# One value piece for two tiles, the scan's decays in two steps, and the last roots on ScalarE and VectorE, in a hybrid decoder trunk on one core

## The chip, the core and the metric

The kernel runs on one core of one Trainium2 chip. The core has five engines with their own instruction streams: TensorE (PE: matmuls, with weight loads shown apart as PEld), VectorE (DVE), ScalarE (ACT), GpSimd (POOL) and SyncE (SP, here only DMA issues). They meet through semaphores. The metric is the device time of one execution in microseconds (us); lower is better. Times shown are medians of several runs, and one further execution is recorded by the hardware profiler.

## What is computed

Two layers over 256 tokens of 1024 columns, then a final RMS norm. A layer normalises its input, multiplies it with one wide matrix `w_in`, runs three mixers on slices of the product (a Mamba-2 scan, attention in a sliding window with sinks, and forgetting attention), gates and projects each, adds the three, projects once more and adds the input. Cut to what the change touches:

```python
# per layer
h = rms_norm(x, norm_w[layer])
proj = jnp.einsum('bsd,de->bse', h, w_in[layer])
... c_q, c_k, c_v, c_f, c_z, gates = jnp.split(proj, split_at, axis=-1)

# the scan, in two chunks of 128 tokens, 16 heads in 4 groups
a_cum = jnp.cumsum(a_dt, axis=-1)
seg = a_cum[..., :, None] - a_cum[..., None, :]
decay = jnp.where(causal, jnp.exp(jnp.where(causal, seg, 0.0)), 0.0)
y_diag = jnp.einsum('bgrcls,bcsgrp->bclgrp', cb[:, :, None] * decay, x_dt)
y_off = jnp.einsum('bclgn,bcgrpn,bgrcl->bclgrp', cc, prev, jnp.exp(a_cum))

# the end
x = x + jnp.einsum('bsd,de->bse', merged, w_out[layer])
return rms_norm(x, final_norm_w)     # x * rsqrt(mean(x * x) + eps) * w
```

## The kernel before

**Precision and pieces.** Every float32 matrix of weights is cut in two: `hi`, rounded to the type fp32r, and `lo`, the rest. A product is the sum of three: activation-high by weight-high, activation-low by weight-high, activation-high by weight-low. Weights come in *pieces* of 256 or 512 columns (`class Piece`), each in *parts* of 512 KB: 4 blocks of 128 rows at 256 columns, or 2 blocks at 512. SyncE loads a part (L356), ScalarE makes its `hi` (L286, or L1389 in the opening stage), VectorE its `lo` (L287, or L1395). At most four parts (`AHEAD`) are split ahead; the next is fed when a matmul loop releases one (`release`, `feed`).

**The two ways through a piece.** The 256 tokens are two tiles of 128. `tok` takes one tile through all 8 row blocks into one bank of accumulators, and is called once for each tile; `tok2` (through `dense2`) takes both tiles by turns, four row blocks of one, four of the other, into two banks. There are three banks of the name mm. For activations that are wanted transposed, `both_sums` makes one *channel* of 128 columns: 8 matmuls of 512 moving columns and 8 of 256.

**Order.** In the opening stage the order on TensorE, VectorE, ScalarE and GpSimd is the program's own. From there on only TensorE's is; on the other engines a planner orders the instructions at compile time, by the order in which the program traces them among those that it takes to be ready. Small stages are generators: `launch` queues one, each `yield` names a delay in the kernel's own estimate of TensorE's time (`clock`, advanced by `mm`), and `pump`, called after each channel or half tile, enters those that are due. A call of `pin` keeps an instruction behind the one traced before it on its engine.

**The scan.** `ssd_group` runs four times in each layer. Its step behind the token "ssd" transposes the inputs on TensorE, scales them (L812), copies B (L817), makes the decays to the chunk's end (L819, L820, L822), then for both chunks four decay rows (L829) and one exponential (L831), and the scaled C (L835, L836). After `D_SSD` the second step multiplies the decays by the products of B and C (L848), and the third does the value products. The first group of a layer comes between channels of the convolution (`u_conv`: an eviction, an accumulating DMA, then `taps` with L773 on ScalarE and three L776 on VectorE, then a tanh L782 and L783) and the first projection.

**The value columns.** In layer one the forgetting attention's values are made by `u_cv`: the first 512 columns are two pieces of 256 (`cv0`, `cv1`), each with two calls of `tok` and an eviction (L956) that scales by the row's norm. They run right behind the opening stage.

**The last norm.** `out_end` adds the input (L1133), sums squares (L242, or on VectorE for the last piece, L1137) and scales by the final weights. For the third piece it makes the variance (L281) and calls `row_rsqrt2`: GpSimd raises it to the power -0.5 (L253), VectorE refines that by one step (L255, L257) and the row is scaled and stored (L1156, L1158).

Of the kernel before, what the change touches and what calls it, by code (L numbers as in the profile page):

```python
# [14 lines left out]
ALU = mybir.AluOpType  # L15
# [6 lines left out]
NEG = -1.0e30  # L22
EPS = 1e-6

D_SOFT, D_SOFT2, D_EVAC, D_SSD, D_SSD2 = 7.0, 3.0, 3.0, 8.0, 4.0
D_K, D_Q, D_QK, D_G0, D_FOX, D_BDMA, D_BIAS, D_BC, D_SSD3 = 6.0, 5.5, 2.0, 8.0, 0.0, 4.0, 2.6, 5.5, 1.0
D_GN1, D_GN2, D_CUM, D_H, D_M = 8.0, 13.5, 12.0, (4.8, 6.4), 5.0
BUDGET = 1.35
# [19 lines left out]
def hybrid_trunk(  # L48
# [198 lines left out]
        ts(v[:, 0:1], v[:, 0:1], 1.0 / D, EPS, op0=ALU.mult, op1=ALU.add)  # L247
        return v

    def row_rsqrt2(v):  # L250

        r0 = T("sm", [P, 8])
        nc.gpsimd.tensor_tensor(r0[:, 0:1], v, mhalf[:, 0:1], op=ALU.pow)  # L253
        a = T("sm", [P, 8])
        stt(a[:, 0:1], r0[:, 0:1], v, r0[:, 0:1], op0=ALU.mult, op1=ALU.mult)  # L255
        r = T("rs", [P, 8], bufs=4)
        stt(r[:, 0:1], a[:, 0:1], -3.0, r0[:, 0:1], op0=ALU.add, op1=ALU.mult)  # L257
        return r
# [540 lines left out]
    def ssd_group(y, g):  # L799
        yield lambda: not any(m[2] == 1 for m in waiting)  # L800
        yield "bcg"
        bcg = T("L4", [P, 4, S])
        nc.scalar.dma_start(bcg, y.cumd[4 * g:4 * g + 4, 0, :].partition_broadcast(P))
        yield D_BC
        yield "ssd"
        xdt = T("L2", [P, 2, 256])
        hs = slice(4 * g, 4 * g + 4)
        for t in range(2):
            p = pmx()
            for j in range(2):  # L810
                transpose(p[:, j * P:(j + 1) * P], y.xs[:, 2 * g + j, t * P:(t + 1) * P], ident)
            tt(xdt[:, t, :].rearrange("p (h d) -> p h d", h=4),  # L812
               p[:, 0:256].rearrange("p (h d) -> p h d", h=4), bc(y.dt[:, t, hs], 2, 64), op=ALU.mult)
        p = pmx()
        transpose(p[:, 0:P], y.bcT[:, g, 0:P], ident)
        bt = T("bt", [P, P])
        act(bt, p[:, 0:P], AF.Copy)  # L817
        ds = T("ds", [P, 4], bufs=2)
        tt(ds, bcg[:, :, P - 1], y.acum[:, 0, hs], op=ALU.subtract)  # L819
        act(ds, ds, AF.Exp)  # L820
        xds = T("L1", [P, 256])
        tt(xds.rearrange("p (h d) -> p h d", h=4), xdt[:, 0, :].rearrange("p (h d) -> p h d", h=4),  # L822
           bc(ds, 2, 64), op=ALU.mult)
        decs = []
        for c in range(2):
            tk = slice(c * P, (c + 1) * P)
            dec = T("L2", [P, 4, P])
            for h in range(4):
                stt(dec[:, h, :], bcg[:, h, tk], y.acum[:, c, 4 * g + h:4 * g + h + 1], negtri,  # L829
                    op0=ALU.subtract, op1=ALU.add)  # L830
            act(dec, dec, AF.Exp)  # L831
            decs.append(dec)

        cx = T("L2", [P, 4, P])
        act(cx, bcg[:, :, P:S], AF.Exp)  # L835
        tt(cx, cx, bc(y.bcT[:, 4 + g, P:S], 1, 4), op=ALU.mult)  # L836
        yield D_SSD
        tokens["bcg"] += 1

        p = pmx()  # L840
        mm(p[:, 0:256], bt, xds, start=True, stop=True)
        for c in range(2):
            tk = slice(c * P, (c + 1) * P)
            mm(p[:, 256 + c * P:384 + c * P], y.bcT[:, g, tk], y.bcT[:, 4 + g, tk], start=True, stop=True)
        st = T("st", [P, 256])
        act(st, p[:, 0:256], AF.Copy)
        for c in range(2):
            tt(decs[c], decs[c], bc(p[:, 256 + c * P:384 + c * P], 1, 4), op=ALU.mult)  # L848
        yield Half(D_SSD2)

        py = pmx()
        for c in range(2):
            for j in range(2):
                o = py[:, S * j + P * c:S * j + P * c + P]
                for s in range(c + 1):
                    for i in range(2):
                        h = 2 * j + i
                        hc = slice(64 * h, 64 * h + 64)
                        a, b = (xdt[:, c, hc], decs[c][:, h, :]) if s == 0 else (st[:, hc], cx[:, h, :])
                        mm(o[64 * i:64 * i + 64, :], a, b, start=(s == 0), stop=(s == c))  # L860
        for j in range(2):
            u = 2 * g + j
            stt(y.xs[:, u, :], y.xs[:, u, :], y.dsk[:, u:u + 1], py[:, S * j:S * j + S], op0=ALU.mult, op1=ALU.add)
        yield D_SSD3
        tokens["ssd"] += 1
# [81 lines left out]
    def u_cv(y, c, t, i=None):  # L947

        def f(w):
            p = tok(y.hTh, y.hTl, w, t)  # L950
            if y.cv is None:
                y.cv = T("L8", [P, 2, D])
            m = w.n if i is None else w.n - 16
            rn = 1.0 if y.rn is None else y.rn[:, t:t + 1]
            if i is None:
                finish(act(halves(y.cv[:, t, c:c + m]), p, AF.Copy, scale=rn))  # L956
            else:
                n = w.n // 2
                act(y.cv[:, t, c:c + n], p[:, 0, :], AF.Copy, scale=rn)
                finish(act(y.cv[:, t, c + n:c + m], p[:, 1, 0:m - n], AF.Copy, scale=rn))  # L960
                logits(y, t, i, p[:, 1, m - n:n])
            pump()
        return f

# [151 lines left out]
    def u_out2(y, c):  # L1116

        def f(w):
            def late():
                drain(8)  # L1120
                limit(None, True)
            drain(7)
            xo = [out_start(y, c, t, 0, w.n) for t in range(2)]
            none = lambda: None
            for t, p in enumerate(tok2(y.mh, y.ml, w, (none, late, none, none))):
                out_end(y, c, t, 0, w.n, xo[t], p)
            state["pin"] = False
        return f

    def out_end(y, c, t, i, n, xo, p):  # L1130
        sl = slice(c, c + n)
        with tc.high_priority():
            tt(halves(y.xn[:, t, sl]), p, halves(xo), op=ALU.add)  # L1133
            last = y.l + 1 == L
            if last and i == 2:
                junk = T("L2", [P, 512])
                nc.vector.tensor_tensor_reduce(out=junk[:, 0:n], in0=y.xn[:, t, sl], in1=y.xn[:, t, sl],  # L1137
                                               scale=1.0, scalar=0.0, op0=ALU.mult, op1=ALU.add,
                                               accum_out=y.ss[t][:, i:i + 1])
            else:  # L1140
                sum_sq(y.xn, t, c, y.ss[t][:, i:i + 1], n)
            nwb = fin["w"] if last else layers[y.l + 1].nwb
            if i == 2:
                v = y.var[t][:, 1:2]
                pin(stt)(v, y.ss[t][:, 2:3], 1.0 / D, y.var[t][:, 0:1], op0=ALU.mult, op1=ALU.add)
            if last:
                pin(stt)(y.xn[:, t, sl], y.xn[:, t, sl], -0.5, nwb[:, sl], op0=ALU.mult, op1=ALU.mult)
            else:
                nc.scalar.dma_start(xres[t * P:(t + 1) * P, sl], y.xn[:, t, sl])
            if i == 1:  # L1150
                y.var[t] = row_var(y.ss[t], 2)
            if i == 2:
                r = row_rsqrt2(v)
                if last:
                    m = 640
                    ts(y.xn[:, t, 0:m], y.xn[:, t, 0:m], r[:, 0:1], None, op0=ALU.mult)  # L1156
                    nc.sync.dma_start(out2[t * P:(t + 1) * P, 0:m], y.xn[:, t, 0:m])
                    act(y.xn[:, t, m:D], y.xn[:, t, m:D], AF.Copy, scale=r[:, 0:1])  # L1158
                    nc.scalar.dma_start(out2[t * P:(t + 1) * P, m:D], y.xn[:, t, m:D])
                else:  # L1160
                    h = layers[y.l + 1].h[t] = T("L4", [P, D])
                    for j in range(2):
                        hs = slice(j * 512, (j + 1) * 512)
                        stt(h[:, hs], y.xn[:, t, hs], r[:, 0:1], nwb[:, hs], op0=ALU.mult, op1=ALU.mult)
        if i == 2 and not last:
            launch(5 + t, hT(layers[y.l + 1], t), D_H[t])
        if i == 1:
            pump()
# [26 lines left out]
    def op(i, *fs):  # L1195
        for f in fs:
            ops.append((i, f))

    for y in layers:
# [10 lines left out]
        def cols(c0, n=256):  # L1210
            return sub([(0, w[:, c0:c0 + n])], n)
# [37 lines left out]

        gp = gates_proj(1)  # L1250
        if l == 0:
            v, cv0, cv1 = cols(C_BV), cols(C_CV), cols(C_CV + 256)
            op(v, *(u_bv(y, t, first) for t in range(2)))
            op(None, lambda: layer_consts(y0, nc.gpsimd))
            op(None, lambda: launch(9, normalize(y0), 0.0))
            op(cv0, u_cv(y, 0, 0), u_cv(y, 0, 1))
            op(cv1, u_cv(y, 256, 0), u_cv(y, 256, 1))
            gp.pop(0)()
            op(None, lambda: tables(fin["rope"]))
            op(None, lambda: normalized(y0))  # L1260
# [253 lines left out]
```

## Time and profile before

| | us |
|---|---|
| median of 3 runs (824.23 to 825.6) | 824.66 |
| the profiled execution | 825.03 |
| its span, first to last instruction | 823.0 |
| busy: TensorE | 811.7 |
| busy: VectorE | 670.6 |
| busy: ScalarE | 550.4 |
| busy: GpSimd | 169.9 |
| moved by DMA | 170.35 MB, mean 207 GB/s |

A row of the timeline or of the chain reads: start, length, engine, line of the kernel, operation, what is written and read (names without their numbers; L, the common prefix, stands for most buffers of SBUF), shapes, and in brackets the idle time before it with what ended it. A row of a group reads: line, engine, operation, names, shapes, count, busy us, mean ns of one, and the idle time before them. Matmuls are pipelined: one that follows another back to back starts before the other ends, so the step from start to start tells what each costs. A line can be a helper's: L106 is every matmul, L110 every transpose, L281 whatever is pinned.

### The profile page before, as it was taken

How to read it: one execution, taken by the hardware profiler on the slowest of the kernel's cores; microseconds unless marked ns; L12 is line 12 of the kernel's file. 1: busy time of each engine (PE TensorE's matmuls, PEld its weight loads, DVE VectorE, ACT ScalarE, POOL GpSimd, SP SyncE). 2: the span in 40 equal slices, each digit the busy share in tenths (PEclk: the TensorE clock that was granted, in tenths of full speed). 3: DMA queues.
4: the chain of work that ended last, by engine and by line, in shares of the span. 5: the costliest groups of instructions: out<-in, count | busy, mean ns of one | idle time of the engine just before them, and what ended most of it. 6: DMA issues, size and time to landing. Idle time of an engine off the chain costs nothing.

```text
span 823.0 us, 15134 instructions
## 1 busy us (share of the span) xinstructions
PE 811.7 (99%) x5266; PEld 724.5 (88%) x5266; DVE 670.6 (81%) x1466; ACT 550.4 (67%) x1198; POOL 169.9 (21%) x234
## 2 busy tenths in 40 slices
PE   9999999999999999999999999999999999999995
PEld 8998988888888888888999898888889889888895
DVE  6879899799898787965776989988889878787664
ACT  7777778685776768543656777877557767684441
POOL 3066113140310010120006621314002210102100
PEclk9999999999999999999999999999999999999998
DMA  9897869697766554865789777969867555467531
GB/s 312 281 257 189 217 183 266 182 246 226 196 180 186 177 169 151 276 207 194 237 270 259 187 205 200 243 186 259 243 196 212 180 169 166 141 205 264 186 113 64
DMA packets 141653, 170.35 MB, mean 207 GB/s; under 512 B 9314, under 2 KB 110298, under 8 KB 141578
## 3 DMA queue, kind: packets, MB, share of 16 engines
q1 hardware_dynamic: 114960, 140.53, 54.7%
q0 software_dynamic: 12928, 12.63, 9.5%
q10 hardware_dynamic: 13690, 16.24, 6.4%
q8 instruction: 41, 0.67, 0.3%
q14 instruction: 34, 0.28, 0.1%
HBM read 154.63 MB, written 2.16 MB: 191 GB/s over the span
## 4 chain that ended last, share of the span: by engine, by line
PE 90%; DVE 5%; issue 2%; ACT 2%; DMA 1%; POOLq 0%; POOL 0%; SPq 0%; ACTq 0%; DVEq 0%
PE mm L106 78%; PE mx L106 7%; PE mx L110 4%; DVE lo L287 1%; DVE L L776 1%; DVE L L829 1%; ACT hi L286 0%; ACT pp L616 0%; DMA L<-in_x_dram 0%; DMA L<-xres 0%; ACT hi L281 0%; DVE pp L610 0%; DVE L L812 0%; DVE L L727 0%; DVE L L836 0%
## 5 line engine op out<-in xcount | busy, mean ns | idle before, releaser
L287 DVE TENSOR_TENSOR lo<-raw,hi 128x1024 fp32r<-128x1024 f32 (+2 forms) x276 | 311.0, 1145 | 55.8 <-ACT hi L286 54.4
L106 PE MATMUL mm<-L,hi 128*128 128x512 f32 x1056 | 353.2, 386 | 0.0
L106 PE MATMUL mm<-hi,L 128*128 128x512 f32 (+2 forms) x1232 | 323.3, 351 | 0.1
L286 ACT ACTIVATE hi<-raw 128x1024 fp32r<-128x1024 f32 (+2 forms) x276 | 264.7, 983 | 55.3 <-PE mm L106 47.5
L106 PE MATMUL mm<-L,lo 128*128 128x256 f32 x1056 | 266.6, 273 | 0.0
L106 PEld LDWEIGHTS mm<-hi,L 128*128 128x128 f32 x1232 | 216.9, 190 | 24.1 <-issue 1.5
L106 PEld LDWEIGHTS mm<-L,hi 128*128 128x128 f32 x1056 | 194.5, 190 | 26.4 <-issue 3.6
L106 PE MATMUL mm<-lo,L 128*128 128x512 f32 (+2 forms) x616 | 213.8, 349 | 0.8 <-DVE lo L287 0.8
L106 PEld LDWEIGHTS mm<-L,lo 128*128 128x128 f32 x1056 | 202.1, 191 | 5.5
L106 PEld LDWEIGHTS mm<-lo,L 128*128 128x128 f32 x616 | 116.3, 190 | 13.1 <-DVE lo L287 1.6
L487 POOL DMA_DIRECT2D L<-L x68 | 59.5, 930 | 182.2 <-ACT L L486 144.8
L616 ACT ACTIVATE pp<-pp,nm 128x128 f32<-128x128 f32 (+1 forms) x128 | 56.6, 445 | 32.8 <-DVE nm L610 32.8
L994 POOL TENSOR_SCALAR_AFFINE_SELECT bias<-bias 128x128 f32<-128x128 f32 x64 | 31.1, 535 | 98.6 <-DMA bias<-cumd 58.6
L776 DVE SCALAR_TENSOR_TENSOR L<-L,vec,L 128x255 f32<-128x255 f32 (+2 forms) x96 | 46.2, 481 | 1.8
L485 ACT ACTIVATE L<-mm 128x256 f32<-128x256 f32 x84 | 31.8, 378 | 17.0 <-PE mm L106 14.1
L1028 ACT ACTIVATE L<-L 128x512 f32<-128x512 f32 x24 | 15.1, 631 | 32.0 <-DVE L L1025 27.8
L628 DVE TENSOR_SCALAR pp<-pp,rsum 128x128 f32<-128x128 f32 (+1 forms) x128 | 32.5, 320 | 0.5
L487 POOL DMA_DIRECT2D qt<-L x16 | 14.5, 990 | 84.3 <-ACT qt L486 46.5
L880 DVE SCALAR_TENSOR_TENSOR L<-L,L 128x256 f32<-128x256 f32 x48 | 21.2, 446 | 9.4 <-ACT L L879 9.1
L647 ACT ACTIVATE L<-mx 128x512 f32<-128x512 f32 x48 | 26.9, 596 | 1.3 <-PE mx L110 1.3
L879 ACT ACTIVATE L<-L 128x256 f32<-128x256 f32 x48 | 19.9, 414 | 10.8 <-DVE L L478 7.5
L1073 POOL TENSOR_TENSOR L<-L,L 128x512 f32<-128x512 f32 x8 | 12.8, 1599 | 68.3 <-DVE L L1072 68.3
(200 smaller groups left out, 848.2 us busy)
## 6 DMA issues: line engine op xcount, KB each, us to landing
raw<-in_w_in_dram SPq DMA_DIRECT2D x191, 512.0 KB, 4.7
raw<-in_w_proj_dram SPq DMA_DIRECT2D x48, 512.0 KB, 5.5
L<-L POOLq DMA_DIRECT2D x72, 128.0 KB, 5.0
raw<-in_w_out_dram SPq DMA_DIRECT2D x16, 512.0 KB, 4.7
bias<-cumd ACTq DMA_DIRECT2D x16, 256.0 KB, 3.8
L<-cumd ACTq DMA_DIRECT2D x8, 512.0 KB, 5.6
L<-in_gate_bias_dram ACTq DMA_DIRECT2D x12, 256.0 KB, 6.1
qt<-L POOLq DMA_DIRECT2D x16, 128.0 KB, 5.3
```

The source lines that it names most:

```text
L106: nc.tensor.matmul(o, a, b, **kw)
L110: nc.tensor.transpose(o, a, i)
L286: keep(act)(hi, src, AF.Copy)
L287: keep(tt)(lo, src, hi.bitcast(F32), op=ALU.subtract)
L485: act(halves(lo), ordered(p[:, S:2 * S]), AF.Copy)
L487: nc.gpsimd.dma_start(out, lo, accum_op=ALU.add)
L616: act(pp[:, i, sl], pp[:, i, sl], AF.Exp, scale=-1.0, bias=nm[:, e:e + 1], accum_out=sums[:, e:e + 1])
L628: ts(pp[:, i, sl], pp[:, i, sl], rs[:, 2 * i + b:2 * i + b + 1], 0.5, op0=ALU.mult, op1=ALU.mult)
L647: act(pT, pt, AF.Copy)
L776: stt(a[:, s:S], x_[:, 0:S - s], y.vec[:, 16 * j + u:16 * j + u + 1], a[:, s:S], op0=ALU.mult, op1=ALU.add)
L880: stt(o, th, 1.0, o, op0=ALU.add, op1=ALU.mult)
L994: nc.gpsimd.affine_select(out=bias[:, i, dst], in_=bias[:, i, src], compare_op=ALU.is_ge, fill=NEG, base=0, pattern=[[-1, P]], channel_mul ...
```

## The change

Three edits. In layer one the first 512 value columns become one piece of 512 for both tiles (`u_cv2`, through `tok2`), evicted once for each tile. In `ssd_group` a `yield D_DEC` stands before the second chunk's decays, and `D_SSD` is shortened by as much (8.0 becomes 2.6 + 5.4); the second chunk's L829 and L831, and L835 and L836 behind them, are traced in the new step. And in the last layer `row_rsqrt2` takes the square root on ScalarE and its reciprocal on VectorE in place of GpSimd's power; a square root of a constant is pinned early in the output projection, which brings ScalarE's table for it.

```diff
-D_SOFT, D_SOFT2, D_EVAC, D_SSD, D_SSD2 = 7.0, 3.0, 3.0, 8.0, 4.0
+D_SOFT, D_SOFT2, D_EVAC, D_DEC, D_SSD, D_SSD2 = 7.0, 3.0, 3.0, 2.6, 5.4, 4.0
...
-    def row_rsqrt2(v):
+    def row_rsqrt2(v, last):
         r0 = T("sm", [P, 8])
-        nc.gpsimd.tensor_tensor(r0[:, 0:1], v, mhalf[:, 0:1], op=ALU.pow)
+        if last:
+            s = T("sm", [P, 8])
+            act(s[:, 0:1], v, AF.Sqrt)
+            nc.vector.reciprocal(r0[:, 0:1], s[:, 0:1])
+        else:
+            nc.gpsimd.tensor_tensor(r0[:, 0:1], v, mhalf[:, 0:1], op=ALU.pow)
...
         decs = []
         for c in range(2):
+            if c == 1:
+                yield D_DEC
             tk = slice(c * P, (c + 1) * P)
             dec = T("L2", [P, 4, P])
...
+    def u_cv2(y):
+        def f(w):
+            ps_ = tok2(y.hTh, y.hTl, w, [pump] * 4)
+            y.cv = T("L8", [P, 2, D])
+            for t, p in enumerate(ps_):
+                finish(act(halves(y.cv[:, t, 0:512]), p, AF.Copy, scale=y.rn[:, t:t + 1]))
+            pump()
+        return f
...
             drain(7)
+            if y.l + 1 == L:
+                pin(act)(tab, ones[:, 0:1], AF.Sqrt)
             xo = [out_start(y, c, t, 0, w.n) for t in range(2)]
...
-                r = row_rsqrt2(v)
+                r = row_rsqrt2(v, last)
...
-            v, cv0, cv1 = cols(C_BV), cols(C_CV), cols(C_CV + 256)
+            v, cv0 = cols(C_BV), cols(C_CV, 512)
...
-            op(cv0, u_cv(y, 0, 0), u_cv(y, 0, 1))
-            op(cv1, u_cv(y, 256, 0), u_cv(y, 256, 1))
+            op(cv0, u_cv2(y))
```

## The prediction

> **What bounds the kernel now.** First the page: the busy shares, the slices, the granted clock.
>
> ```profile
> span 823.0 us, 15134 instructions
> PE 811.7 (99%) x5266; PEld 724.5 (88%) x5266; DVE 670.6 (81%) x1466; ACT 550.4 (67%) x1198; POOL 169.9 (21%) x234
> PE   9999999999999999999999999999999999999995
> PEclk9999999999999999999999999999999999999998
> ```
>
> TensorE is busy in every slice but the last, at full clock. A change is worth only what it takes out of TensorE's own stream, out of a stall of TensorE, or out of the tail after its last matmul. So next the view of who waited for whom, TensorE alone:
>
> ```profile
> engine line waited for: us in total, times, longest us
> PE mx L110 <- POOL ident masks.py:199: 1.5, 1, 1.5
> PE mm L106 <- DVE lo L287: 0.8, 2, 0.5
> PE mx L106 <- DVE nm L610: 0.2, 1, 0.2
> ```
>
> Past the start, TensorE waits for the low half of a weight part (L287) twice in the whole run, and hardly for anything else. The timeline shows both places: the first scan group of each layer.
>
> **Part 1, value columns.** Before, layer one's first 512 value columns are two pieces of 256, and each piece has two tiles of 24 matmuls: 96 matmuls with 256 moving columns. After, one piece with 48 matmuls of 512. The chain of waits, and the groups of the window 20.87 to 36.8 us kept apart by form, price both:
>
> ```profile
> 21.10 15.72 PE mm L106 x96
> 331.29 36.26 PE mm L106 x168
> L106 PE MATMUL mm<-hi,L 128*128 128x256 f32 x32 | 5.5, 278 | 0.0
> L106 PE MATMUL mm<-lo,L 128*128 128x256 f32 x16 | 4.4, 275 | 0.0
> ```
>
> The 168 run back to back at 512 columns: 36.26 / 168 = 0.2158 us each. The window of the 96 holds 32 + 16 = 48 of 256 columns; the other 48 are the gate's 512. So 15.72 - 48 x 0.2158 = 5.36 us for 48 short ones, 0.1117 us each. Then 96 x 0.1117 = 10.72 becomes 48 x 0.2158 = 10.36: **-0.36 us**, all on the path, since TensorE never stops here. The loads are the same four parts of 512 KB, needed in the same order at the same distance (12 long matmuls per two parts, where there were 24 short ones), so the splits and the releases of parts keep their times. Four evictions become two:
>
> ```profile
> 18.45 0.45 ACT L956 ACTIVATE L<-mm,rs 128x256 f32<-128x256 f32 x1
> L647 ACT ACTIVATE L<-mx 128x512 f32<-128x512 f32 x48 | 26.9, 596 | 1.3 <-PE mx L110 1.3
> ```
>
> 4 x 0.45 = 1.8 us of ScalarE becomes about 2 x 0.6 = 1.2, beside TensorE; worth nothing. They come later and both matmul banks are held to the end, but a third bank carries the gate's first tile, 5.2 us of cover; without it the loss would be one eviction, 0.6 us. Bounds: -0.5 to +0.6, taken -0.36.
>
> **Part 2, the scan's decays.** Nothing is removed: eight groups still make 8 L829, two L831, one L835, one L836 each. The second chunk's four L829, its L831, and L835 and L836 are traced one step later. The step waits 2.6; one channel of 16 matmuls adds 8 x (512 + 256) / 2350 = 2.61 to the kernel's own clock, so the step comes one channel later, and the 5.4 behind it ends on the same call as the 8.0 did: TensorE's order stays. What moves is the order on VectorE and ScalarE. The timeline at the first stall:
>
> ```profile
> 177.07 1.08 ACT L286 ACTIVATE hi<-raw 128x1024 fp32r<-128x1024 f32 x1
> 179.38 2.18 DVE L829 SCALAR_TENSOR_TENSOR L<-L,acum,negtri 128x128 f32<-128x128 f32 x8
> 181.08 0.61 ACT L835 ACTIVATE L<-L 128x512 f32<-128x512 f32 x1
> 181.60 0.63 ACT L831 ACTIVATE L<-L 128x512 f32<-128x512 f32 x1
> 181.82 0.68 DVE L836 TENSOR_TENSOR L<-L,L 128x512 f32<-128x512 f32 x1
> 182.13 0.59 ACT L773 ACTIVATE L<-L,vec 128x256 f32<-128x256 f32 x1
> 182.37 0.38 PE L106 MATMUL mm<-lo,L 128*128 128x512 f32 x1
> 182.42 1.21 DVE L287 TENSOR_TENSOR lo<-raw,hi 128x1024 fp32r<-128x1024 f32 x1
> 183.56 0.99 DVE L776 SCALAR_TENSOR_TENSOR L<-L,vec,L 128x255 f32<-128x255 f32 x2
> 183.68 0.48 PE L106 MATMUL mm<-lo,L 128*128 128x512 f32 x1 [0.50 <-DVE lo L287]
> 188.76 1.28 DVE L848 TENSOR_TENSOR L<-L,mx 128x512 f32<-128x512 f32 x2 [0.55 <-ACT st L846]
> ```
>
> The matmuls with a low half step 3 x 0.2158 = 0.65 us. The one due at 182.37 + 0.65 = 183.02 runs at 183.68: 0.66 us lost. Its low half could start when its high half was there (177.07 + 1.08 = 178.15) and started at 182.42, behind eight L829 and L836. Layer two repeats it:
>
> ```profile
> 571.73 2.10 DVE L L829 x8
> 575.06 0.59 PE L106 MATMUL mm<-hi,L 128*128 128x512 f32 x2
> 575.96 0.48 PE L106 MATMUL mm<-lo,L 128*128 128x512 f32 x1 [0.31 <-DVE lo L287]
> ```
>
> The low-half matmul is due two steps of 0.2158 after 575.06, at 575.49, and runs at 575.96: 0.47 lost. **The most that this part can win is 0.66 + 0.47 = 1.13 us**, against a move of 4 x 0.27 + 0.68 = 1.76 us per group.
>
> Does the low half now overtake? The late part is fed on the release that the following channel makes, after the new step is traced; so by trace order the four moved L829 still stand ahead of it. L836 needs L835, now traced late on ScalarE, and may fall behind it: 0.6 won. But between the two steps stand the taps of an earlier channel (L773, then three L776 of 0.99 / 2 = 0.5), which before came behind the burst; now L773 may go ahead of the second L831 and L835, and one or two L776 ahead of the late part: 0.5 to 1.0 lost. I take **0**, the two about cancelling, with ends -1.13 and +3.0 (all three L776 ahead, in both layers). The scan itself has cover: L848 starts at 188.76, 6 us behind L836. If that cover were gone, L848 would be late by what the step moved, 1.76.
>
> **Part 3, the last roots.** TensorE ends at 814.6; the root of the second tile is on the path to the end. From the timeline, and from the groups:
>
> ```profile
> 815.52 0.16 DVE L281 SCALAR_TENSOR_TENSOR sm<-ss,sm 128x1 f32<-128x1 f32 x1
> 815.60 0.42 DVE L281 SCALAR_TENSOR_TENSOR L<-L,nwb 128x256 f32<-128x256 f32 x1
> 815.76 0.67 POOL L253 TENSOR_TENSOR sm<-sm,mhalf 128x1 f32<-128x1 f32 x1 [7.16 <-DVE sm L281]
> 816.47 0.22 DVE L255 SCALAR_TENSOR_TENSOR sm<-sm,sm 128x1 f32<-128x1 f32 x1 [0.45 <-POOL sm L253]
> L622 ACT ACTIVATE es<-es 128x4 f32<-128x4 f32 x16 | 3.1, 194 | 1.2 <-DVE es L620 1.2
> L625 DVE RECIPROCAL rsum<-sums 128x4 f32<-128x4 f32 x32 | 5.6, 176 | 2.5 <-ACT pp L616 2.2
> ```
>
> Before: the variance is there at 815.52 + 0.16 = 815.68, and L255 starts at 816.47, 0.79 later. After: the same hop of 0.08 to another engine, then an ACTIVATE of 0.2 (the narrow one, 0.194), so 815.96; VectorE is in its 256-column L281 until 816.02; the reciprocal takes 0.18; L255 at about 816.22: **-0.25 us**. Bounds: -0.35 if nothing overlaps badly, 0 if each hop costs 0.15 more. The first tile's root has TensorE for cover. ScalarE must also load another table, early in the output projection:
>
> ```profile
> 1.46 1.28 ACT L183 ACT_TABLE_LOAD   x1 [1.46 <-PEq L1503]
> 2.75 0.20 ACT L183 ACTIVATE tab<-tab 128x1 f32<-128x1 f32 x1
> 792.84 0.60 ACT L289 ACTIVATE L<-mx 128x512 fp32r<-128x512 f32 x1 [3.43 <-PE mx L110]
> 795.96 0.60 ACT L281 ACTIVATE L<-mx 128x512 fp32r<-128x512 f32 x1 [2.52 <-PE mx L110]
> ```
>
> It is pinned behind the 792.84 split, which ends at 793.44; 1.28 + 0.20 ends at 794.92, inside ScalarE's idle 2.52 us before 795.96: nothing. The row at 1.46 shows the ACTIVATE 1.29 after the load's start, with no drain behind it, though nothing was in flight there. The Trainium skill (ScalarE: Activation LUTs, What ACT_TABLE_LOAD costs) speaks against that: it counts some 2.66 us for a switch of sets, a drain of 1.38 included. By that rule the sum would be 0.34 us worse; this trace has no switch under load.
>
> **The sum.** -0.36 + 0 - 0.25 = -0.61 us. The profiled execution took 825.03 us (823.0 of span, 2.0 around it), 0.37 above the median of 824.66; from the median, 824.05 us.
>
> **The rivals.** (a) *The burst really opens*: the late part overtakes the moved L829 in both layers, and both stalls go. For: 1.76 moved against 0.66 and 0.47. Against: the trace order above. 824.05 - 1.13 = 822.9. (b) *The taps step in*: L773 goes ahead of the second exponentials, all three L776 ahead of the late part, and the low half comes 3 x 0.5 = 1.5 later in each layer: 824.05 + 3.0 = 827.05, slower than before; in one layer with one or two of the L776 it is 824.55 to 825.05. For: VectorE has no idle time between the L829 and L836 of the timeline, so whatever goes ahead is paid in full. Against: the taps wait for their own accumulating DMA. It decides from the point where more L776 go ahead (0.5 each) than L836 behind (0.6). (c) *The table load is not hidden*: if it waits for the split in flight and so stands for two of its rows, ScalarE is free at 793.44 + 2 x 1.28 + 0.20 = 796.20, the split of 795.96 starts 0.24 late, and TensorE, whose last matmuls before the second piece need that split, with it: 824.3. For: the one load of the trace had nothing before it. Against: the gap of 2.52 holds the 1.48 of the rows. The page named above has the same mechanism. (d) *The planner's new order elsewhere* (six more groups, where no stall is now) makes a stall like the 0.66: 824.7, or twice 825.4.
>
> **How the numbers follow.** Forecast 0.45, with 823.6 to 824.6 as its own range; (a) 0.24; (b) 0.16, a quarter of it in full; (c) 0.07; (d) 0.08. A measurement of this kernel tells about 0.2%, 1.65 us, from no change: below 823.0 counts as faster, above 826.3 as slower. (a) lands at 822.9, just beyond the bound; two thirds of it count, which with a little from the forecast's edge makes 0.18. The full (b) and double mishaps give 0.08 slower, and 0.74 remain. The range 822.7 to 825.6 leaves out the far half of (a) and the full (b).
>
> **What would show it.** Right: 48 matmuls of 512 in the stage after 15 us, and what follows 0.3 to 0.4 us earlier; at 183 and 575 a wait for L287 of about the same length; L255 some 0.55 us after the variance; one table load, between 793.4 and 796. Wrong: no wait for L287 in TensorE's waits (a), or waits of over 1 us with L776 ahead of the low half (b); a split at 796 that starts behind the load (c). The forecast is wrong as a whole if the span changes by more than 1.7 us, since no stall of that size is there to be won.

## The result: slower by 0.57%, and the profile after

| | before | after |
|---|---|---|
| median, runs on one chip, us | 824.46 (823.76 to 826.98) | 830.32 (828.43 to 831.76) |
| ratio | | 1.0057, 95% interval 1.0044 to 1.0070 |
| the profiled execution; its span | 825.03; 823.0 | 830.8; 829.0 |
| from the start of TensorE's last matmul to the end of the span | 8.74 | 6.68 |

The ratio says 0.57%, that is 4.7 us; the medians of the runs shown are 5.9 us apart, just beyond the upper end of the interval (5.8). A gain of 0.6 us had been forecast. Lines of before stand lower in the changed kernel: L287 (low half) is L292, L773 and L776 (taps) are L778 and L781, L782 (tanh) is L787, L803 (the broadcast of a scan group) is L808, L819 is L824, L829 is L837, L831 is L839, L835 and L836 are L843 and L844, L848 is L856. The page's first lines and TensorE's own list of waits, whose columns are what waited, for whom, us in total, times and the longest:

```profile
span 829.0 us, 15040 instructions
PE 814.8 (98%) x5218; PEld 724.3 (87%) x5218; DVE 671.1 (81%) x1468; ACT 551.0 (66%) x1200; POOL 170.3 (21%) x232
```

```profile
PE mm L106 <- DVE lo L292: 3.2, 2, 2.2
PE mx L106 <- DVE L L856: 1.4, 2, 1.0
```

TensorE has 48 matmuls fewer, and is busy longer. The wait for a low half is no longer 0.8 us but 3.2, and a wait for the scan's L856 is new. The start of the same matmul in the two traces says where each microsecond came in:

| time in before | after is later by, in all | what stands there |
|---|---|---|
| 26.30 | -0.38 | end of the value stage |
| 117.7 | +0.22 | matmuls of the decay logits, layer one |
| 173.4 | +0.83 | transposes of the second scan group |
| 183.7 | +1.32 | low half of part four, layer one |
| 190.8 | +1.79 | value products of the scan, layer one |
| 421 | +2.48 | two short waits (0.54), and 0.16 right behind the value products |
| 510 | +3.09 | matmuls of the decay logits, layer two |
| 575.96 | +5.14 | low half of part four, layer two |
| 578.0 | +6.81 | the matmuls right behind it |
| 583.1 | +7.90 | value products, layer two |
| 814.3 | +8.06 | last matmul |
| end | +6.0 | |

The steps at the decay logits (0.60 and 0.61) are no larger than the scatter: in c_pool below, which has neither the new value piece nor the decays in two steps, the same places bring +0.61 at 117 and -0.54 at 510. The heavy place is layer two's first scan group, 4.8 us in three steps (2.05, 1.67, 1.09). The timeline of after there, engine by engine:

```profile
576.70 0.63 ACT L839 ACTIVATE L<-L 128x512 f32<-128x512 f32 x1 [0.57 <-DVE L L837]
578.79 0.60 ACT L778 ACTIVATE L<-L,vec 128x256 f32<-128x256 f32 x1 [1.46 <-DMA L<-L]
579.30 0.61 ACT L843 ACTIVATE L<-L 128x512 f32<-128x512 f32 x1
579.82 0.61 ACT L839 ACTIVATE L<-L 128x512 f32<-128x512 f32 x1
...
580.87 2.00 ACT L291 ACTIVATE hi<-raw 128x1024 fp32r<-128x1024 f32 x2
582.61 0.37 ACTq L808 DMA_DIRECT2D L<-cumd  x1
...
577.19 0.87 DVE L837 SCALAR_TENSOR_TENSOR L<-L,acum,negtri 128x128 f32<-128x128 f32 x3
579.43 0.48 DVE L781 SCALAR_TENSOR_TENSOR L<-L,vec,L 128x255 f32<-128x255 f32 x1 [1.37 <-ACT L L778]
579.83 1.22 DVE L292 TENSOR_TENSOR lo<-raw,hi 128x1024 fp32r<-128x1024 f32 x1
...
590.16 0.16 DVE L824 TENSOR_TENSOR ds<-L,acum 128x4 f32<-128x4 f32 x1 [4.52 <-DMA L<-cumd]
590.24 1.28 DVE L856 TENSOR_TENSOR L<-L,mx 128x512 f32<-128x512 f32 x2
...
578.32 0.59 PE L106 MATMUL mm<-hi,L 128*128 128x512 f32 x2
581.10 0.63 PE L106 MATMUL mm<-lo,L 128*128 128x512 f32 x1 [2.19 <-DVE lo L292]
590.97 1.04 PE L106 MATMUL mx<-L,L 128*64 128x128 f32 x12 [1.01 <-DVE L L856]
```

Read it in two chains. **The first**: the tap's L778 now stands ahead of L843 and of the second L839 on ScalarE, and waits there 1.46 us for its accumulating DMA. VectorE has the first L781 ahead of the low half L292 and waits with it, 1.37. The low-half matmul was due at 578.32 + 2 x 0.2158 = 578.75 and runs at 581.10: 2.35 lost, where before lost 0.47. **The second**: the next group's broadcast L808 writes where L837 and L843 read; L843 ends at 579.91. The issue of the broadcast stands in ScalarE's own order behind two weight splits (L291) and comes at 582.61 (574.00 before). The next L824 stands ahead of L856 on VectorE in both kernels; now it holds VectorE for 4.52 us until the broadcast lands, and the value products wait for L856. The chain that ended last holds both transfers, each with its own length:

```profile
571.95 6.83 DMA L<-L
582.61 7.53 DMA L<-cumd
```

Between the two stands a third loss. The windows of after around the standstill (columns: the window, the engines' busy time, granted clock of TensorE, DMA share, GB/s):

```profile
578.75:581.10 2.35, 0.16 (x2) 0.00 (x1) 1.67 (x3) 2.31 (x6) 0.00 (x0) 1.00 0.29 52
581.10:584.40 3.30, 3.30 (x11) 2.76 (x11) 3.30 (x6) 2.07 (x3) 0.86 (x1) 0.53 0.63 174
```

Behind 2.19 us in which TensorE stood idle (the wait for L292 above) the clock is granted at 0.53 for 3.3 us: 3.3 x 0.47 = 1.55 us more, most of the step of 1.67 in the table.

### The profile page after: what moved, and what is told of

Its sections match the earlier page's. It is cut to its first block, busy times and chain, and to the rows that moved or that the text cites. A ratio compares the mean times of both kernels' runs of the same rounds, so it can differ in the third digit from the quotient of the medians.

```text
span 829.0 us, 15040 instructions
## 1 busy us (share of the span) xinstructions
PE 814.8 (98%) x5218; PEld 724.3 (87%) x5218; DVE 671.1 (81%) x1468; ACT 551.0 (66%) x1200; POOL 170.3 (21%) x232
## 4 chain that ended last, share of the span: by engine, by line
PE 65%; ACT 10%; DMA 8%; DVE 8%; issue 6%; POOL 2%; ACTq 0%; POOLq 0%; DVEq 0%
PE mm L106 57%; PE mx L106 6%; DMA L<-cumd 4%; PE mx L110 3%; DMA L<-L 3%; ACT hi L291 3%; ACT pp L621 2%; DVE lo L292 2%; DVE L L781 1%; DMA bias<-cumd 1%; ACT L L778 1%; DMA L<-in_x_dram 1%; POOL L L492 1%; ACT L L490 1%; ACT L L491 1%
## 5 line engine op out<-in xcount | busy, mean ns | idle before, releaser
L292 DVE TENSOR_TENSOR lo<-raw,hi 128x1024 fp32r<-128x1024 f32 (+2 forms) x276 | 310.6, 1144 | 55.1 <-ACT hi L291 53.5
L291 ACT ACTIVATE hi<-raw 128x1024 fp32r<-128x1024 f32 (+2 forms) x276 | 263.5, 981 | 55.6 <-PE mm L106 45.7
L106 PEld LDWEIGHTS mm<-hi,L 128*128 128x128 f32 x1200 | 213.6, 190 | 25.5 <-issue 1.5
L106 PE MATMUL mm<-lo,L 128*128 128x512 f32 (+2 forms) x600 | 211.5, 354 | 3.2 <-DVE lo L292 3.2
L106 PEld LDWEIGHTS mm<-lo,L 128*128 128x128 f32 x600 | 113.3, 190 | 15.9 <-DVE lo L292 4.0
L781 DVE SCALAR_TENSOR_TENSOR L<-L,vec,L 128x255 f32<-128x255 f32 (+2 forms) x96 | 46.1, 481 | 3.3 <-ACT L L778 1.5
```

What stands on the lines that cost most here:

```text
L106: nc.tensor.matmul(o, a, b, **kw)
L291: keep(act)(hi, src, AF.Copy)
L292: keep(tt)(lo, src, hi.bitcast(F32), op=ALU.subtract)
L781: stt(a[:, s:S], x_[:, 0:S - s], y.vec[:, 16 * j + u:16 * j + u + 1], a[:, s:S], op0=ALU.mult, op1=ALU.add)
```

## The experiments

Ratios are to the kernel before on the same chip, with 95% intervals.

| run | what it is | median (before) | ratio |
|---|---|---|---|
| a_only | value piece alone | 826.3 (825.64) | 1.0013, 1.0003 to 1.0023 |
| b_only | decays in two steps alone | 830.87 (825.64) | 1.0070, 1.0053 to 1.0086 |
| c_only | roots alone | 823.22 (825.64) | 0.9973, 0.9963 to 0.9984 |
| ac | the change without the two steps | 824.79 (825.64) | 0.9990, 0.9981 to 0.9998 |
| a_pad | a_only, 48 short transposes at the start | 828.57 (825.17) | 1.0047, 1.0031 to 1.0062 |
| c_pool | c_only and a copy by GpSimd | 825.57 (825.17) | 1.0003, 0.9995 to 1.0012 |
| b_cxe | b_only, L835 in the first step | 826.09 (825.17) | 1.0009, 1.0000 to 1.0019 |
| c_mul52 | c_only, L836 alone in a later step | 822.08 (825.17) | 0.9963, 0.9950 to 0.9976 |
| acm | c_mul52 and the value piece | 823.08 (825.47) | 0.9972, 0.9961 to 0.9983 |
| c_d52_cxe | c_only, second step after two channels | 823.71 (825.47) | 0.9975, 0.9966 to 0.9984 |

**One part at a time.** The three edits, each by itself, and the first with the third:

```diff
 a_only
-            v, cv0, cv1 = cols(C_BV), cols(C_CV), cols(C_CV + 256)
+            v, cv0 = cols(C_BV), cols(C_CV, 512)
...
 b_only
+            if c == 1:
+                yield D_DEC
...
 c_only
+            act(s[:, 0:1], v, AF.Sqrt)
+            nc.vector.reciprocal(r0[:, 0:1], s[:, 0:1])
...
 ac, against the changed kernel
-            if c == 1:
-                yield D_DEC
```

> Before with the value piece alone. Theory (order): TensorE leaves the value stage 0.36 to 0.38 us earlier, and the wait for the decay logits of layer one (about 117 us) takes that back, so 0 to -0.4 us against before. Rival (the value piece disturbs the planner's order and is the cause of the loss): +4 to +6 us.

> Before with the decays in two steps alone. Theory: ScalarE runs L773, which waits for its accumulating DMA, ahead of the second exponentials, so the low half comes later and TensorE stands at the first scan group of each layer: +6 to +9 us against before, with waits of over 1 us for L287 in both layers and L819 late for its DMA. Rival (the value piece is the cause): 0 to +1 us.

> Before with the last roots alone. Theory: L255 0.25 us earlier, and GpSimd's closing drain, which ends 5.8 us after its last instruction, no longer ends the run: -1.9 to -2.2 us against before. Rival (only the shorter root counts): -0.2 to -0.3 us.

> The changed kernel with the decays put back into one step. Theory: -1.9 to -2.5 us against before, so some 8 us below the changed kernel. Rival (the value piece is the cause): still +3 to +6 us above before.

The two steps alone cost as much as the whole change, the roots gain 2.4 us, and the value piece, which saves 0.36 us of matmuls, costs 1.1 to 1.4 by the ratios (a_only against before, and ac against c_only: 0.9990 to 0.9973). The ratios add up: 0.13 + 0.70 - 0.27 = 0.56%, against 0.57 for the whole. The medians do not (3.5 us against 5.9), so totals here are good to a microsecond or two and not to tenths. Three expectations missed: a_only lost 0.7 us where up to 0.4 was to be gained, ac gained 0.9 in place of 1.9 to 2.5, and b_only lost 5.2 in place of 6 to 9.

b_only also shows that the two chains of the section above are two. TensorE's waits of b_only, and its clock behind the longest:

```profile
PE mx L106 <- DVE L L850: 3.6, 2, 2.6
PE mm L106 <- DVE lo L287: 1.5, 1, 1.5
```

```profile
590.20:593.60 3.40, 3.40 (x15) 2.53 (x12) 3.40 (x5) 2.11 (x3) 0.00 (x0) 0.51 0.50 140
```

Here the low half waits long only in layer one; in layer two the accumulating DMA landed before L773 came up. What hurts is the second chain: 2.6 us for L850 (L848 of before), and again a clock of about one half for 3.4 us.

**The two chains taken apart.** In b_cxe the exponential of the scaled C moves back into the first step; the second chunk's decays and L836 stay in the second.

```diff
             act(dec, dec, AF.Exp)
             decs.append(dec)
-        cx = T("L2", [P, 4, P])
-        act(cx, bcg[:, :, P:S], AF.Exp)
+            if c == 0:
+                cx = T("L2", [P, 4, P])
+                act(cx, bcg[:, :, P:S], AF.Exp)
```

> The kernel before with the two steps of decays alone, but the exponential of the scaled C (L835) in the first step, behind the first L831. Theory (two losses, of two causes): the value products of the scan come late (about 0.5 to 1 us at 191 and 1.1 to 2.6 at 583) because the next group's broadcast, which writes where L835 and L829 read, is issued 4.8 to 8.6 us later and the next L819 stands ahead of L848 in VectorE's order; with L835 early the broadcast is issued at most 2.5 us later than before and that part goes. The low half of part four stays late by 0.5 to 1 us at 184 and about 2 at 576, since one L776 with its wait for an accumulating DMA still stands ahead of it. Total 2 to 3.5 us slower than before, against 5.2 with L835 in the second step. Rival (the standstill at the low half alone makes the rest): 5 us slower as before.

Measured 0.9 us slower than before, where 2 to 3.5 had been expected. The timeline of b_cxe in layer two (L831 is L829 of before):

```profile
576.06 0.60 ACT L773 ACTIVATE L<-L,vec 128x256 f32<-128x256 f32 x1 [0.49 <-DMA L<-L]
576.38 0.37 ACTq L803 DMA_DIRECT2D L<-cumd  x1
...
575.68 0.60 DVE L831 SCALAR_TENSOR_TENSOR L<-L,acum,negtri 128x128 f32<-128x128 f32 x2
...
576.81 0.47 DVE L776 SCALAR_TENSOR_TENSOR L<-L,vec,L 128x255 f32<-128x255 f32 x1
577.21 1.21 DVE L287 TENSOR_TENSOR lo<-raw,hi 128x1024 fp32r<-128x1024 f32 x1
582.33 0.15 DVE L819 TENSOR_TENSOR ds<-L,acum 128x4 f32<-128x4 f32 x1
```

The broadcast is issued at 576.38, 0.1 after the last L831 (575.68 + 0.60), and L819 has no idle time before it: the second chain is gone, and with it the steps of TensorE at 191 and 583. The first is still there, smaller than expected: L773 waits 0.49 us and one L776 stands ahead of the low half, which costs TensorE 0.26 us more than before at 184 and 0.70 at 576. No standstill is long enough for the clock to fall. Of b_only's 5.2 us, 4.3 went with the late broadcast and the half clock that its standstill brought; what the low halves cost is about the same in both profiles (0.9 us in b_only, 1.0 here). The edit moves more than L835: on ScalarE one weight split now stands ahead of the second exponential, and on VectorE the multiplication of the scaled C (L839) stands ahead of the first L776. How much the first chain takes depends on when the accumulating DMA lands, 6.83 us after its issue in the changed kernel, 5.09 in b_only and 5.86 in b_cxe.

**Only what harms nobody, moved.** c_mul52 keeps all readers of the broadcast and all exponentials where they were, and puts off L836 alone, by two channels.

```diff
-D_SSD = 8.0
+D_DEC, D_SSD = 5.2, 2.8
...
         act(cx, bcg[:, :, P:S], AF.Exp)
+        yield D_DEC
         tt(cx, cx, bc(y.bcT[:, 4 + g, P:S], 1, 4), op=ALU.mult)
```

> The kernel before with the new roots, and of the decays only the multiplication of the scaled C (L836, 0.68 us) moved to a step of its own, two channels later (5.2 of the 8.0). All readers of the broadcast, the exponentials and the 8 L829 stay. Theory (what stands on VectorE ahead of the low half decides, and the taps' wait is the harm): the low half of part four goes ahead of L836, TensorE's two waits for it (0.66 and 0.47 us) go or fall below 0.2, nothing else moves, and the run is 0.8 to 1.1 us faster than the one with the roots alone: 3.2 to 3.5 us faster than before. Rival 1 (any step put off brings the taps in and costs): slower than the roots alone by 0.5 or more. Rival 2 (the low half is bound by its own high half or by TensorE's half-rate after a stall): within 0.3 of the roots alone.

822.08 us, by its median the fastest of all, 3.1 us under before. Its timeline at layer two's low half (L842 is L836 of before):

```profile
574.31 1.22 DVE L292 TENSOR_TENSOR lo<-raw,hi 128x1024 fp32r<-128x1024 f32 x1
575.84 0.68 DVE L842 TENSOR_TENSOR L<-L,L 128x512 f32<-128x512 f32 x1
...
575.00 0.59 PE L106 MATMUL mm<-hi,L 128*128 128x512 f32 x2
575.58 0.48 PE L106 MATMUL mm<-lo,L 128*128 128x512 f32 x1
```

The low half has overtaken L842, and its matmul, due at 575.00 + 0.43 = 575.43, loses 0.15 in place of 0.47; in layer one 0.29 in place of 0.66. So the idea of the change, to let the low half through, is worth 0.7 us of TensorE against this trace of before. In c_only, c_pool and a_pad, whose decays are unmoved too, the two matmuls lose 0.42 to 0.55 and 0.35 to 0.43, and against these it is about 0.5. The totals do not tell c_mul52 from c_only (their intervals overlap). c_mul52 also has a loss of its own: the layer's first broadcast is read 7.68 us after its issue, against 5.6 to 6.4 in the other kernels but acm (7.54), and TensorE loses 0.4 us right behind it, at 168. The cause of that stays open.

The other way to let it through is to put the second step behind part four. c_d52_cxe is c_only with b_cxe's edit and these delays:

```diff
-D_DEC, D_SSD = 2.6, 5.4
+D_DEC, D_SSD = 5.2, 2.8
```

> The kernel before with the new roots and the decays in two steps, but the second step after two channels (5.2 + 2.8 in place of 2.6 + 5.4) and the exponential of C (L835) in the first: the low half of part four stands right behind the first four L829, ahead of the second four, of L836 and of the taps' three L776. Theory (two places on one path): both waits for the low half go, as where only L836 was moved; but the second L829 now end behind two L776, the next broadcast, which writes where they read, is issued 3 to 4 us later than before (181.7), and the next L819, ahead of L848 on VectorE, waits for it 1 to 3 us; the value products at 191 and 583 lose 0 to 2 us each. 0 to 3 us slower than the run with L836 alone moved (822.08): ratio 0.9965 to 1.0. Rival (the low half is all that matters): within 0.3 us of that run, no wait of L819.

```profile
572.53 1.21 DVE L292 TENSOR_TENSOR lo<-raw,hi 128x1024 fp32r<-128x1024 f32 x1
582.18 0.16 DVE L824 TENSOR_TENSOR ds<-L,acum 128x4 f32<-128x4 f32 x1 [2.06 <-DMA L<-cumd]
```

The low half comes even earlier (572.53) and its matmul loses nothing in either layer. But the next broadcast is issued later again (576.36, against 574.21 in c_mul52), L824 waits 2.06 us for it, and TensorE loses 1.38 us at 583. What the first chain gives, the second takes: the total is that of c_only (0.9975 and 0.9973).

**The new roots.** c_pool adds an instruction of GpSimd that nobody waits for.

```diff
             nc.vector.reciprocal(r0[:, 0:1], s[:, 0:1])
+            nc.gpsimd.tensor_copy(s[:, 4:5], r0[:, 0:1])
```

> The kernel before with the new roots alone, and behind each of them a copy of one column by GpSimd that nobody reads. The path of the root is that of the run with the roots alone (823.22 beside 825.64, so 2.4 us faster). Theory (GpSimd's end): its closing DRAIN ends about 5.8 us after its last instruction and the execution waits for it; with an instruction of GpSimd there again, 1.5 to 1.8 us of the gain go, and the run is 0.4 to 1.0 us faster than the kernel before. Rival (the root's own path is the gain, or the store): 2.1 to 2.4 us faster as without the copy.

The whole gain is gone, more than expected: 1.0003 against 0.9973. GpSimd's closing DRAIN shows why, in the rows for the kernel's last line (three DRAINs: shortest, median and longest in ns, first and last start in us). Before (with the row of SyncE, which waits for the stores), c_only, c_pool:

```profile
L1510 POOLq DRAIN  x3: 46/93/6512, 815.7 to 822.7; - x3
L1510 SPq DRAIN  x3: 7/7/7, 820.4 to 822.5; - x3
```

```profile
L1518 POOLq DRAIN  x3: 46/98/7951, 762.5 to 821.2; - x3
```

```profile
L1519 POOLq DRAIN  x3: 46/93/6004, 815.6 to 822.1; - x3
```

The first DRAIN is the long one, and it starts with GpSimd's last instruction. Before, that is the power of the second tile (815.76, 0.67 long): it ends at 816.43 and the DRAIN at 815.7 + 6.5 = 822.2. In c_pool the copy ends at 815.75, the DRAIN at 821.6. In c_only the last instruction ends at 764.63 and the DRAIN at 770.5. Each time the DRAIN ends 5.8 us after the last instruction, and in before and c_pool the end of the execution waits for it: SyncE's first DRAIN of before is at 820.4, 1.8 us before GpSimd's ends. The copy of c_pool waits for the new root and ends 2.14 us after the start of the last matmul, the power of before 2.15, so there the shorter root wins nothing. From the start of the last matmul to the end of the span: before 8.74, c_pool 8.73, c_only 6.64, the changed kernel 6.68.

**The value piece.** Both a_only and ac lose about 0.6 us at 173, behind the second broadcast, and 0.4 to 0.5 more than before at the low half at 184. a_pad gives TensorE's stream as many instructions as before:

```diff
             transpose(warm[:, 0:P], ident, ident)
+        for i in range(48):
+            transpose(warm[:, 0:NK], ident[:NK, :], ident[:NK, :NK])
```

> The kernel before with the one value piece of 512 columns alone, and 48 narrow transposes (8 columns each, of a constant) more in TensorE's stream before its first input: as many instructions as the 48 matmuls that the piece saves. The total is later by what these take at the start and is not what is read. Theory (the place of the instruction fetch): in the three runs with the piece, a 16 KB packet of the instruction queue starts at 164.0 to 164.6 us, among the packets of the two broadcasts (L803) issued at 158.6 to 159.8, and the second one is read (L819) 9.7 to 9.8 us after its issue; in the three runs without it the packet starts at 155.4 to 157.3, before the broadcasts are issued, and L819 comes 8.6 to 9.0 after. With the stream as long as before the packet is ahead of the broadcasts again, L819 comes 8.6 to 9.0 us after the issue, and the step of 0.4 to 0.7 us on TensorE at 173 goes. Rival (the piece itself: its loads, its two late evictions, or that what follows comes 0.3 us earlier): 9.7 us and the step stay.

The DMA view of 2 us (share: of 16 DMA engines), then the second broadcast's issue and its reader in the timeline. Before, from 154.9 to 156.9:

```profile
q8 instruction: 1, 0.02, 3.0%
```

```profile
159.59 0.38 ACTq L803 DMA_DIRECT2D L<-cumd  x1
168.30 0.16 DVE L819 TENSOR_TENSOR ds<-L,acum 128x4 f32<-128x4 f32 x1 [1.28 <-DMA L<-cumd]
```

a_only, from 163.5 to 165.5:

```profile
q10 hardware_dynamic: 372, 0.37, 54.9%
...
q8 instruction: 1, 0.02, 3.0%
```

```profile
159.31 0.38 ACTq L803 DMA_DIRECT2D L<-cumd  x1
169.02 0.17 DVE L819 TENSOR_TENSOR ds<-L,acum 128x4 f32<-128x4 f32 x1 [1.75 <-DMA L<-cumd]
```

a_pad, from 159.3 to 161.3:

```profile
q8 instruction: 1, 0.02, 3.2%
```

```profile
163.63 0.38 ACTq L803 DMA_DIRECT2D L<-cumd  x1
172.13 0.16 DVE L819 TENSOR_TENSOR ds<-L,acum 128x4 f32<-128x4 f32 x1 [0.98 <-DMA L<-cumd]
```

One packet of instructions takes 3.0% of 16 engines for 2 us, 0.96 us of a single engine. In a_only it falls among the packets of the broadcasts (q10), and L819 follows the issue by 9.71 us; in before and a_pad it is over before the broadcasts are issued, and L819 follows by 8.71 and 8.50. In a_pad TensorE's steps at 173 and 184 are absent, and the value stage is still 0.36 us shorter; the total is longer because the 48 transposes took 4.2 us at the start. The pair shows that the 1 us hangs on the length of TensorE's stream and not on the piece itself. That the packet is the link is read from the times: in the four kernels with the piece and no padding it starts at 163.9 to 164.6 and the read follows the issue by 9.7 to 10.0 us, in seven others it is over before the issue and the read follows by 8.5 to 9.0. c_mul52 fits neither group (packet at 157.0, 9.3 us), behind its late first broadcast, so a packet is not the only thing that delays a read here; whether the packet held up the engine that the broadcast needed is not shown. acm asks what the piece does on the best version:

```diff
 c_mul52, and
+            op(cv0, u_cv2(y))
```

> The changed kernel with only the multiplication of the scaled C (L836) in the later step, two channels on, as in the run that had it with the new roots (822.08 beside 825.17: ratio 0.9963): so that run plus the one value piece of 512 columns. Theory (the piece saves 0.36 us on TensorE, but shifts the instruction fetch into the first broadcasts, and the two waits that this lengthens are at 173 and at the low half of part four): the fetch packet starts at about 164, the second broadcast is read 9.7 us after its issue, TensorE loses 0.6 at 173; at 184 the low half now has 0.6 us of slack, so less than 0.3 is lost there. 0 to 0.7 us slower than that run, ratio 0.996 to 0.9975. Rival (the piece is worth its 0.36 once the low half has slack): 0.3 to 0.5 us faster than that run.

It costs 0.7 us there too (0.9972 against 0.9963, intervals overlapping); the packet is back among the broadcasts, L824 follows the issue by 9.96 us, and TensorE loses 0.50 at 174. The low half loses 0.2 more than in c_mul52, less than 0.3 as expected.

## Why the prediction was wrong

The step that failed most is part 2's "I take **0**": by itself the part measured +5.2 us. Part 1's -0.36 became a loss of about 1 us, and part 3's -0.25 was a gain of over 2.

**What bounds the kernel** was read rightly: every loss but the tail's is a stall of TensorE, or the lower clock behind one. But "no stall of that size is there to be won" looked only at what could be won; a stall that a reordering can make has no such bound.

**Part 1**, "-0.36 us, all on the path, since TensorE never stops here": the stage itself is 0.36 us shorter, as forecast, 15.13 to 26.30 before and 15.11 to 25.92 after (the first long matmul behind it, before and after):

```profile
26.30 0.60 PE L106 MATMUL mm<-hi,L 128*128 128x512 f32 x2
```

```profile
25.92 0.59 PE L106 MATMUL mm<-hi,L 128*128 128x512 f32 x2
```

What failed is the step from the stage to the end: 48 matmuls fewer also move every later instruction packet, here by 8.6 us and, as the times above are read, into a transfer that TensorE waits for 140 us later. In a_only's profile the steps are 0.6 us at 173, 0.4 at 184, and 0.2 each at 510 and 576, the last two within the scatter: about -0.36 + 1.4.

**Part 2**, "I take 0, the two about cancelling". The order of rival (b), which had been given 0.16 and at most 3.0 us, came: L773 ahead of the second exponentials in both layers, and of the three L776 one ahead of the low half. Its mark, "waits of over 1 us with L776 ahead of the low half", is there. Three things were wrong in the working. First, "Against: the taps wait for their own accumulating DMA" was read as a reason why they would not step in. The orders here are fixed at compile time by an estimate, and a wait at run time does not move the waiting instruction back: it blocks all that follows on its engine (1.46 us on ScalarE, 1.37 on VectorE). That argument held the size of the loss, not a reason against it. Second, the sum followed L836 and the low half, and not the release of the broadcast's buffer: "The scan itself has cover: L848 starts at 188.76, 6 us behind L836" is true of L836, but L848 came late through L819, which stands ahead of it and waits for a broadcast issued 8.6 us later in layer two (4.8 in layer one, 186.52 against 181.72). Some 3 and 1 us of this are the general lag; the rest is the new order. In layer two the last exponential that reads the buffer ends 5.9 us later than before (579.91, against 573.97), and the issue stands another 2.7 us behind it in ScalarE's order. b_cxe, in which the broadcast is early again, keeps 0.9 of b_only's 5.2 us. Third, no price was put on the clock behind a standstill, 1.55 us. So the end of +3.0 was too near: b_only measured +5.2.

That part 2 could win at most 1.13 us holds: of this c_mul52 won 0.69 at the two low halves, and c_d52_cxe all of it, which its second chain took back.

**Part 3**, "-0.25 us". The root's own path, in the timeline of after:

```profile
823.57 0.16 DVE L286 SCALAR_TENSOR_TENSOR sm<-ss,sm 128x1 f32<-128x1 f32 x1
823.77 0.20 ACT L255 ACTIVATE sm<-sm 128x1 f32<-128x1 f32 x1 [2.35 <-DVE sm L286]
824.00 0.16 DVE L256 RECIPROCAL sm<-sm 128x1 f32<-128x1 f32 x1
824.20 0.22 DVE L260 SCALAR_TENSOR_TENSOR sm<-sm,sm 128x1 f32<-128x1 f32 x1
```

0.47 us from the variance (823.73) to L260, against 0.55 forecast and 0.79 before: that working was right to 0.1 us. But the term was mis-sized, 2.1 to 2.4 us in place of 0.25, since the end of before did not hang on the root: it hung on GpSimd's DRAIN, and the trace of before had the row. With GpSimd still in the tail the new root gains nothing (c_pool); with GpSimd out of it the tail is 2.1 us shorter, 1.8 of them the DRAIN.

Rival (c), the table load, is answered as forecast; the timeline of after:

```profile
801.51 1.28 ACT L286 ACT_TABLE_LOAD   x1
802.81 0.20 ACT L286 ACTIVATE tab<-ones 128x1 f32<-128x1 f32 x1
804.01 0.60 ACT L286 ACTIVATE L<-mx 128x512 fp32r<-128x512 f32 x1 [1.00 <-PE mx L110]
```

The ACTIVATE that goes with it starts 1.30 us after the load, as in the row at 1.46 before, though now a split stands right ahead of the load. It ends at 803.01, and ScalarE still idles 1.00 us for TensorE before the next split. Rival (d) gave a few tenths: the cause of the 0.54 us in two steps at 412 and 421 stays open.

## What to carry to other kernels

Before an instruction is traced later, list what it releases (here the buffer of the next broadcast) and what gets ahead of it on its engine; the buffer's next writer and that writer's first reader belong to the sum, and a wait that moves ahead of others is paid by all of them. At the end of a kernel look at the closing DRAINs before shortening a chain there: here GpSimd's, 5.8 us behind its last instruction, cost nothing where that instruction was 50 us earlier, and a copy of 0.18 us on it cost some 2. A saving of instructions moves the instruction packets behind it, so a gain or loss of a microsecond far from the edit is to be looked for in the DMA view too.

## What was not expected of the hardware

- **Half clock after a short standstill.** 2.19 us of waiting brought 0.53 of the clock for 3.3 us (after), 2.6 us of waiting 0.51 for 3.4 us (b_only); waits of 1.0 us (b_cxe) and 1.5 us (b_only, layer one) brought nothing. The Trainium skill (TensorE: Matmul & The Clock Gate, What's actually happening) has the clock fall after an idle window of about 3.4 us and come back after as long a busy one. The traces agree on the way back; the fall came after less, and the measurement decides.
- **GpSimd's end.** Its closing DRAIN ended 5.8 us after its last instruction in all three kernels above, whether that was a power, a copy or a 512-column addition.
- **Instruction packets among the data.** The Trainium skill (Runtime: NRT & Kernel Launch, Instruction fetch mechanics) tells of refills in blocks of 16 KiB whose cost is mostly hidden. The rows agree on the block (1 packet of 0.02 MB). The cost seen here is not TensorE's own: a broadcast issued shortly before such a packet was read 1 us later.
